# A feed-forward's row of 1/rms(x): spread over the partitions by two TensorE matmuls instead of two DMAs through DRAM, with the first gates issued one group of column tiles earlier

## The chip, the cores and the metric

The kernel runs on one core of one Trainium2 chip. The metric is the device time of one execution in microseconds (us); three runs of the kernel before gave a median of 2030.98 us. A difference is called one only when it is above about 0.2% of that.

## The reference

The reference is a trunk of four layers on x of 256 tokens x 1024 features. Each layer is a half-step SwiGLU feed-forward, a token mixer and another half-step feed-forward. Mixers alternate: chunked attention (layers 0 and 3), a gated MLP (layer 1), differential attention (layer 2). All is float32. The part that matters here is the feed-forward, which occurs eight times:

```python
def rms_norm(x, g):
    y = xf * lax.rsqrt(jnp.mean(xf * xf, axis=-1, keepdims=True) + EPS)
    return (y * g.astype(jnp.float32)).astype(x.dtype)
def swiglu(h, w_in, w_out):            # w_in 1024 x 5632, w_out 2816 x 1024
    gate, up = jnp.split(h @ w_in, 2, axis=-1)
    return (jax.nn.silu(gate) * up) @ w_out
x = x + 0.5 * rms_norm(swiglu(rms_norm(x, g[0]), ff1_w_in[i], ff1_w_out[i]), g[1])
```

## The kernel before, in words

**Layout.** x lies in SBUF transposed: features on the 128 partitions in 8 tiles (`KD`), 256 tokens along the columns. A product h @ w is made column tile by column tile: the weights (128 x 128 blocks) are the stationary operand, h with 256 columns the moving one. To keep float32 accuracy with the fast float32r type, each operand is split into a high and a low part and three matmuls are made for each block: high x high, high x low, low x high.

**The weights' stream** (class `Stream`, lines 87 to 161). Weights come in the order of use in chunks of 1 MB (tile `w_raw`, three buffers, DMAs issued on SP, line 104). A chunk holds two *pieces*; a piece is one column tile for all 8 k, 8 blocks. Each piece is split: ScalarE (ACT) casts its high part `w_hi` (line 127) and VectorE (DVE) subtracts to give its low part `w_lo` (line 130); the low part of a piece is issued only when the next piece is split (`settle`). Eight buffers of split pieces exist. `W.done(n, most)` says that n pieces were used and lets the stream split up to `most` further pieces, so that a piece is normally split eight pieces ahead of its use. A chunk's DMA is issued when the chunk three earlier has had both its pieces split. Between two branches the stream is held (`hold`, `resume`); in front of a feed-forward that follows a mixer it has split three pieces fewer than in front of one that follows another feed-forward.

**Order.** TensorE, DVE and ACT run their instructions in the order in which the program issues them (`manual_schedule`); a wait at the head of one of them holds back everything behind it on that engine. So the place of a call in the program sets the order.

**The norm.** `Normed` (line 248) multiplies x by the gain only; the factor 1/rms(x), one number per token, is applied later, to the products. `sums` (line 321) makes the sums of squares with small matmuls (`column_sums`, line 225), a square root on ACT (line 233) and a reciprocal on DVE (line 235); the result `rs` has tokens on the partitions, 128 x 2. The products have tokens along the columns, so the factor must be spread as a row over all partitions (tile `rbc`). There are two ways. `spread` (line 327) transposes and broadcasts by matmuls with the identity (`spread2`, line 240) into PSUM and copies the row to SBUF on ACT (line 331); attention uses it. `spread_later` (line 333) writes the 256 numbers to DRAM (tile `row`, line 337) and reads them back onto all 128 partitions (line 338), both DMAs issued on POOL; the feed-forward and the gated MLP use it.

**The feed-forward** (`ffn`, line 511). The first product has 22 gate tiles and 22 up tiles. The loop over `jp` (0 to 10) takes a group of two gate and two up tiles, i = 0 to 3, in `project_pair` (line 471): 24 matmuls for each i, 96 for a group (group 0, after an update of x, is made in another order, line 482, and partly ahead). A group's results fill one PSUM tile `pp_t` of a pool with three buffers, so group 3 can only start when `gate` of group 0 has read the buffer. After the matmuls of each i, `between(i)` is called and then `W.done(1, 2)`, which issues the splits of further pieces.

`gate` (line 521) is a chain of five instructions: DVE multiplies the gate tiles by `rbc` (line 523), ACT applies Silu (line 524), DVE multiplies by the up tiles, which is the last read of the PSUM tile (line 526), ACT casts the high part of the hidden layer (line 528) and DVE makes the low part (line 529). The second product (lines 551 to 563) follows the loop.

In the kernel before, `sums` and `spread_later` are called in group 1 after i = 0; groups 0 and 1 are kept in `held`, and their gates are issued in group 2 after i = 1 and i = 2. From group 2 on each gate is issued right after its group.

Of the kernel before, what the change touches and what calls it, by code (L numbers as in the profile page):

```python
# [16 lines left out]
P = 128  # L17
# [19 lines left out]
# an input that comes in tile by tile: its high parts, and a tile later its low parts  # L37


def _order(ks):  # L40
    """The products' two steps for each k, the one of the input's low part a k behind."""
    steps = [(k, low) for k in ks for low in (False, True)]
    for i in range(1, len(steps) - 1, 2):
        steps[i], steps[i + 1] = steps[i + 1], steps[i]
    return steps
# [3 lines left out]
# After an update of x: first the tiles of which nothing is made ahead.  # L49
# [7 lines left out]
def encoder_trunk_kernel(  # L57
# [29 lines left out]
    class Stream:  # L87
        """Chunks of 16 blocks (128 x 128) in the order of use; a piece is half a chunk."""
# [43 lines left out]
        def settle(self):  # L132
            # the low part follows a piece later, so that its engine need not wait for the high part
            if self.pending:
                self.low(*self.pending)
                self.pending = None
# [74 lines left out]
    class Warm:  # L211
        """Matmuls whose result nobody reads, to keep the tensor engine's clock up while it waits."""
# [17 lines left out]
    def inv_sqrt(src, bias, n, scale):  # L230
        """1 / sqrt(scale * src + bias) of n columns."""
        sd = small.tile([P, n], F32, tag=f"sd{n}", name="sd")
        nc.scalar.activation(sd, src, AF.Sqrt, bias=bias, scale=scale)
        r = small.tile([P, n], F32, tag=f"rs{n}", name="rs")
        nc.vector.reciprocal(r, sd)
        return r

    def spread(col, ps):
        # ps[p, t] = col[t] on every partition p
        nc.tensor.matmul(ps, col.broadcast_to([P, P]), ident, start=True, stop=True)  # L240
# [7 lines left out]
    class Normed:  # L248
        """x * gain in float32r parts, with 1/rms(x) kept aside, per token."""
# [35 lines left out]
        def begin(self, gain):  # L285
            """x itself comes in, and with it the first weights."""
            for k in range(KD):
                self.high(gain, k, k + 1)
                self.low(gain, k, k + 1)
                if k == 0:  # L290
                    W.split()
            for i in range(3):
                W.split()
                W.settle()
                for a in ((0, 2, 4), (6,), ())[i]:
                    self.square(a)
            self.total()
# [29 lines left out]
        def spread(self):  # L327
            """The same on all partitions, for tokens along the columns."""
            ps = spread2(self.tok)
            self.bc = tmp.tile([P, S], F32, tag="rbc", name="rbc", bufs=1)  # L330
            nc.scalar.copy(self.bc, ps)

        def spread_later(self):
            """The same by way of DRAM, where it may take some microseconds."""
            row = dram.tile([S], F32, tag="row", name="row")
            self.bc = tmp.tile([P, S], F32, tag="rbc", name="rbc", bufs=1)
            nc.gpsimd.dma_start(row.rearrange("(h p) -> p h", h=2), self.tok)
            nc.gpsimd.dma_start(self.bc, row.unsqueeze(0).broadcast_to([P, S]))

    class Branch:  # L340
        """A branch's output y, tile by tile: y * gain, and the sum of squares."""

        def __init__(self, gain, n=None, ahead=None):
            """n: the normed input whose 1/rms y still lacks; eps then goes with the square of that rms."""
            self.gain, self.n, self.ahead = gain, n, ahead
# [23 lines left out]
        def finish(self):  # L369
            """The updates of x."""  # L370
            f = inv_sqrt(self.ss[:, 0:2], eps2_t if self.n else eps_t, 2, 1.0 / D)
            self.fill(8)
            fb = spread2(f)
            self.fill(36 if self.ahead else 12)
            return Update(self.yg, f, fb, self.ahead)

    class Ahead:
        """Some of the next products, of x and of y apart, made while y's factor f is on its way: (x + f y) w."""
# [28 lines left out]
        def begin(self):  # L407
            """The first tile of the next products, and apart from it y's share."""
            self.ps, self.share = pair(), bank()
            for o, xs in ((self.ps[:, 0, :], self.x), (self.share, self.y)):  # L410
                for k in self.ks:
                    if self.wide:
                        wh, wl = [part.rearrange("p (k c) -> p k c", k=2)[:, k % 2, :] for part in W.peek(k // 2)]
                    else:
                        wh, wl = [part[:, k, :] for part in blocks(W.peek())]
                    for m, (w_, h) in enumerate(((wh, 0), (wl, 0), (wh, 1))):
                        x = xs[k][:, h, :]
                        first, last = (k, m) == (self.ks[0], 0), (k, m) == (self.ks[-1], 2)
                        self.todo.append((o, w_, x, first, last and o is self.share))
# [10 lines left out]
        def scale(self, update):  # L430
            """y's share, times the factor."""
# [12 lines left out]
    class Update:  # L444
        """x += y * factor, tile by tile."""
# [16 lines left out]
    def large(tag, shape, dtype=F32):  # L462
        """A part of the two arrays of the feed-forward's hidden layer, or what a mixer keeps there."""
        t = act.tile([P, LARGE[tag]], dtype, tag=tag, name=tag)
        n = math.prod(shape)
        return t[:, 0:n].rearrange("p (a b) -> p a b", a=shape[0]) if len(shape) > 1 else t[:, 0:n]
# [4 lines left out]
    def project_pair(n, together, between=lambda piece: None, finish=lambda ps: None, most=2, warm=None):  # L471
        """Two tiles of two column sets each; all four at once where the input comes in k by k."""
# [38 lines left out]
    def ffn(l, which, update, ahead):  # L511
# [21 lines left out]
        def between(jp):  # L533
            def at(i):
                if jp == 1 and i == 0:
                    n.sums(AF.Silu)
                    n.spread_later()
                if jp == 2 and i > 0 and held:
# [3 lines left out]
        for jp in range(NJ // 2):  # L542
            ps = project_pair(n, jp == 0 and not first, between(jp), **(dict(most=1, warm=Warm()) if first and jp == 0 else {}))
            if jp < 2:
# [23 lines left out]
    def project_out(parts, l, between, ahead):  # L568
        """y = o @ w. parts(k): o's float32r parts; between(k): what else is to be done before the k-th is used."""
# [33 lines left out]
    def joined(early, outs):  # L603
        """The float32r parts of a mixer's output, tiles 0 to 3 and 4 to 7 in different places."""
# [4 lines left out]
    class Wide:  # L609
        """Columns of h @ w with tokens on the partitions, 512 columns at a time, a piece (2 of 8 k) per step."""  # L610
# [35 lines left out]
    # Columns of a map: queries 0-127 x keys 0-127, queries 128-255 x keys 128-255, queries 128-255 x keys 0-127.  # L646
# [20 lines left out]
    def soft_exp(s, scale):  # L667
        """exp(scale * (s - max)) for each row of each map, and their sums: [P, map, query half]."""
# [20 lines left out]
    def transpose_probs(p, dst):  # L689
        """p's blocks -> keys 0-127 x queries 0-255, keys 128-255 x queries 128-255."""  # L690
# [5 lines left out]
    def attention(n, softmax, transposes, v_done, mix, prepare=lambda: None, soon=lambda: None):  # L696
        """v's first half, q and k, the maps of each two tiles, and v's other half, with no wait of the tensor engine."""
# [17 lines left out]
        def quarter(i, j):  # L715
            # while the projections of the next two tiles, or of v, go on
# [43 lines left out]
    def mixer_a(l, i, update):  # L760
# [65 lines left out]
        def mix(j):  # L826
            # the heads of v's first 512 columns while the others are made
# [6 lines left out]
        def between(k):  # L834
            # the rest of the heads while the first ones' share of the output is made
# [18 lines left out]
    def mixer_b(l, i, update):  # L854
# [56 lines left out]
        def mix(jp):  # L911
            # rows of v mixed in their chunk, for two of the groups
# [46 lines left out]
    def mixer_c(l, i, update):  # L959
# [9 lines left out]
        # |q - k| on the blocks  # L969
# [7 lines left out]
        # lambda  # L977
# [18 lines left out]
        def softmax(h, sc):  # L996
# [8 lines left out]
            def finish():  # L1005
                # the first map's sums stay in, and come out with the norm: its eps takes their squares
# [21 lines left out]
        def apply(g):  # L1028
            # two heads, tokens on the partitions
# [14 lines left out]
        def summed(g):  # L1044
            # the sums of its squares
# [5 lines left out]
        def normed(g):  # L1051
            # the group over its root mean squares
# [18 lines left out]
        def mix(j):  # L1071
            # the heads of v's first 512 columns while the others are made
# [11 lines left out]
        def between(k):  # L1084
            # the rest of the heads while the first ones' share of the output is made
# [40 lines left out]
def _lay_out(i):  # L1126
    """The inputs in the order in which the chip reads them."""
# [5 lines left out]
    def narrow(w):  # L1133
        # [1024, 1024] -> chunks of two column tiles: [p, 2 * k * 128]
        return w.reshape(KD, P, KD // 2, 2, P).transpose(2, 1, 3, 0, 4).reshape(-1, P, WC)

    def wide(w):
        # [1024, 1024] -> chunks (column half, k half): [p, 4 * 512]
        return w.reshape(2, 4, P, 2, 512).transpose(3, 0, 2, 1, 4).reshape(-1, P, WC)

    def two(w, tiles):
        # [1024, 2 * tiles * 128] -> chunks of a tile of either half: [p, 2 * k * 128]
        return w.reshape(KD, P, 2, tiles, P).transpose(3, 1, 2, 0, 4).reshape(-1, P, WC)

    def deep(w):
        # [2816, 1024] -> blocks (column tile, k), 16 to a chunk
# [17 lines left out]
    # relative-position bias, Toeplitz: same 128-block, and the block before  # L1164
# [34 lines left out]
```

## Time and profile before

| | |
|---|---|
| median of three runs (lowest to highest) | 2030.98 us (2030.81 to 2031.15) |
| span of the profiled execution | 2036.8 us |
| ACT busy, DVE busy | 1076.5 us (53%), 1276.6 us (63%) |
| POOL busy | 16.9 us (1%) |
| mean granted TensorE clock | 0.989 |
| HBM read | 348.49 MB, 172 GB/s over the span |

The profile is one execution taken by the hardware profiler. Its page gives the busy time of each engine (PE is TensorE's matmuls, PEld its weight loads), the chain of work that ended last, groups of instructions by line, and DMAs by size and time to landing. The trace behind it can be asked for waits (who waited for whom), for a timeline of single instructions (start, duration, and in brackets the idle time before and who ended it), and for stretches of time (busy time of each engine, granted clock, busy share of the 16 DMA engines, GB/s). A matmul's shown duration includes its way through the pipeline; the pace of a series of matmuls is read from their starts.

### The profile page before, as it was taken

How to read it: one execution, taken by the hardware profiler on the slowest of the kernel's cores; microseconds unless marked ns; L12 is line 12 of the kernel's file. 1: busy time of each engine (PE TensorE's matmuls, PEld its weight loads, DVE VectorE, ACT ScalarE, POOL GpSimd, SP SyncE). 2: the span in 40 equal slices, each digit the busy share in tenths (PEclk: the TensorE clock that was granted, in tenths of full speed). 3: DMA queues.
4: the chain of work that ended last, by engine and by line, in shares of the span. 5: the costliest groups of instructions: out<-in, count | busy, mean ns of one | idle time of the engine just before them, and what ended most of it. 6: DMA issues, size and time to landing. Idle time of an engine off the chain costs nothing.

```text
span 2036.8 us, 37668 instructions
## 1 busy us (share of the span) xinstructions
PE 1986.9 (98%) x16195; PEld 1956.4 (96%) x16195; DVE 1276.6 (63%) x1689; ACT 1076.5 (53%) x1602; POOL 16.9 (1%) x37
## 2 busy tenths in 40 slices
PE   8999999899999999899999999989999999998998
PEld 8999999899999989899999999989999999998998
DVE  5655766655565567655666558766556655866653
ACT  5554665545454555545554555754545455565442
POOL 0000000000000000000000000000000000000000
PEclk9999999999999999999999999999999999999999
DMA  8545525554554553654464544265447454526541
GB/s 252 187 186 188 188 102 144 214 202 169 146 209 182 191 168 125 192 204 174 158 188 182 191 148 166 104 185 204 174 146 196 186 198 166 188 104 170 199 193 42
DMA packets 51142, 351.96 MB, mean 173 GB/s; under 512 B 6144, under 2 KB 6400, under 8 KB 9760
## 3 DMA queue, kind: packets, MB, share of 16 engines
q1 hardware_dynamic: 48096, 341.86, 48.7%
q10 hardware_dynamic: 2160, 6.52, 0.9%
q8 instruction: 126, 2.06, 0.4%
q0 software_dynamic: 720, 1.19, 0.3%
q14 instruction: 40, 0.33, 0.0%
HBM read 348.49 MB, written 1.06 MB: 172 GB/s over the span
## 4 chain that ended last, share of the span: by engine, by line
PE 88%; DMA 6%; DVE 3%; ACT 2%; issue 1%; ACTq 0%; SPq 0%; DVEq 0%
PE pp_t L501 46%; PE pp_t L166 9%; PE pp_t L168 9%; PE pp_t L167 9%; DMA w_raw<-in_w 6%; PE pp_t L482 3%; PE pp_t L621 3%; PE pp_t L579 2%; DVE w_lo L130 1%; ACT w_hi L127 1%; PE pp_t L661 1%; PE pp_t L427 1%; PE pst_t L693 1%; PE pst_t L427 1%; PE pst_t L225 1%
## 5 line engine op out<-in xcount | busy, mean ns | idle before, releaser
L127 ACT CAST w_hi<-w_raw 128x1024 fp32r<-128x1024 f32 (+1 forms) x649 | 668.2, 1047 | 545.9 <-PE pp_t L501 242.2
L130 DVE TENSOR_TENSOR w_lo<-w_raw,w_hi 128x1024 fp32r<-128x1024 f32 (+1 forms) x649 | 773.5, 1218 | 272.0 <-ACT w_hi L127 254.0
L501 PE MATMUL pp_t<-xh,w_hi 128*128 128x256 f32 x2976 | 533.2, 286 | 35.2 <-DVE hf L526 33.9
L501 PE MATMUL pp_t<-xl,w_hi 128*128 128x256 f32 x2976 | 529.1, 285 | 0.2 <-DVE xl L316 0.2
L501 PE MATMUL pp_t<-xh,w_lo 128*128 128x256 f32 x2976 | 528.6, 285 | 0.0
L501 PEld LDWEIGHTS pp_t<-xh,w_hi 128*128 128x128 f32 x2976 | 435.7, 194 | 38.3 <-issue 35.3
L501 PEld LDWEIGHTS pp_t<-xl,w_hi 128*128 128x128 f32 x2976 | 436.0, 194 | 0.5 <-DVE xl L316 0.4
L501 PEld LDWEIGHTS pp_t<-xh,w_lo 128*128 128x128 f32 x2976 | 435.8, 194 | 0.1
L166 PE MATMUL pp_t<-h,w_hi 128*128 128x256 f32 x1456 | 412.1, 283 | 0.0
L167 PE MATMUL pp_t<-h,w_lo 128*128 128x256 f32 x1456 | 412.1, 283 | 0.0
L168 PE MATMUL pp_t<-l,w_hi 128*128 128x256 f32 x1440 | 407.6, 283 | 0.0
L167 PEld LDWEIGHTS pp_t<-h,w_lo 128*128 128x128 f32 x1456 | 279.6, 192 | 0.0
L166 PEld LDWEIGHTS pp_t<-h,w_hi 128*128 128x128 f32 x1456 | 279.6, 192 | 0.0
L168 PEld LDWEIGHTS pp_t<-l,w_hi 128*128 128x128 f32 x1440 | 276.5, 192 | 0.0
L363 DVE TENSOR_TENSOR ysq<-ysq,sq 128x256 f32<-128x256 f32 x72 | 30.5, 424 | 128.4 <-ACT sq L352 128.3
L523 DVE TENSOR_TENSOR gs<-pp_t,rbc 128x512 f32<-128x512 f32 x88 | 60.5, 688 | 77.7 <-PE pp_t L501 77.7
L526 DVE TENSOR_TENSOR hf<-pp_t,gs 128x512 f32<-128x512 f32 x88 | 60.9, 692 | 68.1 <-ACT gs L524 68.1
L524 ACT ACTIVATE gs<-gs 128x512 f32<-128x512 f32 x88 | 55.6, 632 | 84.0 <-DVE gs L523 84.0
L529 DVE TENSOR_TENSOR l<-hf,h 128x512 fp32r<-128x512 f32 x88 | 60.9, 692 | 60.4 <-ACT h L528 60.4
L528 ACT CAST h<-hf 128x512 fp32r<-128x512 f32 x88 | 54.5, 620 | 66.6 <-DVE hf L526 66.6
L301 ACT ACTIVATE xh<-xr,g_sb 128x256 fp32r<-128x256 f32 x96 | 44.8, 504 | 59.0 <-DVE xr L458 56.4
L678 ACT ACTIVATE ex<-s,nm 128x128 f32<-128x128 f32 x96 | 42.7, 448 | 43.5 <-DVE nm L670 25.3
(191 smaller groups left out, 1706.4 us busy)
## 6 DMA issues: line engine op xcount, KB each, us to landing
w_raw<-in_w SPq DMA_DIRECT2D x322, 1024.0 KB, 4.9
l<-in_a_bias ACTq DMA_DIRECT2D x8, 512.0 KB, 7.5
w_raw<-in_w SPq DMA_DIRECT2D x3, 512.0 KB, 7.2
rbc<-row POOLq DMA_DIRECT2D x9, 128.0 KB, 7.3
out_y<-xr SPq DMA_DIRECT2D x4, 256.0 KB, 2.5
xr<-in_x_t SPq DMA_DIRECT2D x2, 384.0 KB, 5.4
w_raw<-in_w SPq DMA_DIRECT2D x2, 256.0 KB, 4.4
l<-in_b_ws ACTq DMA_DIRECT2D x1, 512.0 KB, 5.4
```

What stands on the lines that cost most here:

```text
L127: nc.scalar.copy(hi[:, cols], raw[:, cols])
L130: nc.vector.tensor_tensor(lo[:, cols], raw[:, cols], hi[:, cols].bitcast(F32), op=ALU.subtract)
L166: nc.tensor.matmul(o, ah, bh, start=start, stop=False, skip_group_check=skip)
L167: nc.tensor.matmul(o, al, bh, start=False, stop=False, skip_group_check=skip)
L168: nc.tensor.matmul(o, ah, bl, start=False, stop=stop, skip_group_check=skip)
L482: nc.tensor.matmul(o, part[:, k, :], (n.l if low else n.h)[:, k, :], start=((k, low) == JOIN[0] and i == 2 and part is ws[i][0]), stop=((k ...
L501: nc.tensor.matmul(o, part[:, k, :], xs[:, k, :], start=(at == 0), stop=(at == 3 * KD - 1))
L523: nc.vector.tensor_tensor(gs, ps[:, :, 0:S], n.bc.unsqueeze(1).broadcast_to([P, 2, S]), op=ALU.mult)
L524: nc.scalar.activation(gs, gs, AF.Silu)
L526: nc.vector.tensor_tensor(hf, ps[:, :, S:2 * S], gs, op=ALU.mult)
L529: nc.vector.tensor_tensor(hl, hf, hh.bitcast(F32), op=ALU.subtract)
L621: nc.tensor.matmul(self.ps[:, t, :], xs[:, kk, t * P:(t + 1) * P], ws, start=((kk, low) == self.order[0] and ws is wh and not (t == 0 and ...
```

## The change

In the feed-forward alone, `spread` takes the place of `spread_later`, one i later, in group 1; the gate of group 0 is issued in group 1 after i = 2; the gate of group 1 is issued right after its group, as all later ones are. The gated MLP keeps `spread_later`. The diff's other lines take out comments and docstrings and are left out here; a line of the changed kernel behind line 537 stands one lower than before.

```diff
         def between(jp):
             def at(i):
                 if jp == 1 and i == 0:
                     n.sums(AF.Silu)
-                    n.spread_later()
-                if jp == 2 and i > 0 and held:
+                if jp == 1 and i == 1:
+                    n.spread()
+                if jp == 1 and i == 2:
                     gate(*held.pop(0))
             return at
...
             ps = project_pair(n, jp == 0 and not first, between(jp), **(dict(most=1, warm=Warm()) if first and jp == 0 else {}))
-            if jp < 2:
+            if jp == 0:
                 held.append((jp, ps))
             else:
                 gate(jp, ps)
```

The two helpers that change places, unchanged themselves:

```python
        def spread(self):
            ps = spread2(self.tok)      # two matmuls into PSUM: ps[p, t] = tok[t] on every p
            self.bc = tmp.tile([P, S], F32, tag="rbc", name="rbc", bufs=1)
            nc.scalar.copy(self.bc, ps)

        def spread_later(self):
            row = dram.tile([S], F32, tag="row", name="row")
            self.bc = tmp.tile([P, S], F32, tag="rbc", name="rbc", bufs=1)
            nc.gpsimd.dma_start(row.rearrange("(h p) -> p h", h=2), self.tok)
            nc.gpsimd.dma_start(self.bc, row.unsqueeze(0).broadcast_to([P, S]))
```

## The prediction, made before the changed kernel was run

> **What bounds the kernel now.** I read the page first, then the waits of TensorE.
>
> ```profile
> PE 1986.9 (98%) x16195; PEld 1956.4 (96%) x16195; DVE 1276.6 (63%) x1689; ACT 1076.5 (53%) x1602; POOL 16.9 (1%) x37
> ```
> ```profile
> PE pp_t L501 <- DVE hf L526: 33.9, 8, 6.9
> ```
> ```profile
> PE pp_t L501 <- ACT w_hi L127: 1.3, 1, 1.3
> ```
>
> The first row says that TensorE sets the time almost everywhere, so an edit is worth what it takes out of or puts into TensorE's row. The second (us in total, times, longest) is nearly all of TensorE's idle time: eight waits, one for each feed-forward, for line 526, the last read of a group's PSUM tile. Group 3 waits for group 0's buffer. The third is the only wait of these products for a weight, 1.3 us at the kernel's start.
>
> Next, why line 526 is late: the timeline of one feed-forward (layer 1's second), TensorE, then ACT, then DVE; start, duration, idle time before in brackets.
>
> ```profile
> 819.66 1.12 PE L501 MATMUL pp_t<-xh,w_lo 128*128 128x256 f32 x8
> 820.62 1.12 PE L501 MATMUL pp_t<-xh,w_hi 128*128 128x256 f32 x8
> ```
> ```profile
> 836.94 1.12 PE L501 MATMUL pp_t<-xh,w_lo 128*128 128x256 f32 x8
> 843.30 0.55 PE L501 MATMUL pp_t<-xh,w_hi 128*128 128x256 f32 x1 [5.25 <-DVE hf L526]
> ```
> ```profile
> 819.41 2.94 ACT L127 CAST w_hi<-w_raw 128x1024 fp32r<-128x1024 f32 x3
> 822.60 2.00 ACT L127 CAST w_hi<-w_raw 128x1024 fp32r<-128x1024 f32 x2 [0.25 <-DMA w_raw<-in_w]
> 834.15 2.00 ACT L127 CAST w_hi<-w_raw 128x1024 fp32r<-128x1024 f32 x2 [9.55 <-DMA w_raw<-in_w]
> 837.73 1.99 ACT L127 CAST w_hi<-w_raw 128x1024 fp32r<-128x1024 f32 x2 [1.59 <-DMA w_raw<-in_w]
> 840.22 1.04 ACT L127 CAST w_hi<-w_raw 128x1024 fp32r<-128x1024 f32 x1 [0.50 <-DMA w_raw<-in_w]
> 841.80 0.63 ACT L524 ACTIVATE gs<-gs 128x512 f32<-128x512 f32 x1 [0.54 <-DVE gs L523]
> ```
> ```profile
> 818.13 0.17 DVE L235 RECIPROCAL rs<-sd 128x2 f32<-128x2 f32 x1 [0.38 <-ACT sd L233]
> ...
> 820.49 5.77 DVE L130 TENSOR_TENSOR w_lo<-w_raw,w_hi 128x1024 fp32r<-128x1024 f32 x5 [1.08 <-ACT w_hi L127]
> ```
> ```profile
> 842.46 0.69 DVE L526 TENSOR_TENSOR hf<-pp_t,gs 128x512 f32<-128x512 f32 x1 [0.69 <-ACT gs L524]
> ```
>
> A step of TensorE takes 0.12 us (eight from 819.66 to 820.62). Groups 1 and 2 run without a gap until 836.94 + 0.96 = 837.90. Group 0's products were there before group 1 began, but its Silu stands on ACT behind twelve casts of weights (two ahead of these rows), the last five of which waited for DMA; 842.46 + 0.69 = 843.15 frees the buffer. Gate 0 is held by its place in the queue, behind weights that TensorE does not need yet.
>
> Why were the weights late there? Stretches of time (the last three columns: granted clock, DMA busy share, GB/s), with a stretch of the first attention, which spreads its row by matmuls:
>
> ```profile
> 822.00:825.00 3.00, 3.00 (x27) 3.00 (x27) 3.00 (x3) 2.35 (x3) 0.00 (x0) 1.00 1.46 44
> 825.00:828.00 3.00, 3.00 (x27) 3.00 (x27) 1.26 (x2) 0.00 (x0) 0.00 (x0) 1.00 0.90 41
> 828.00:831.00 3.00, 3.00 (x27) 3.00 (x27) 0.00 (x0) 0.00 (x0) 0.57 (x1) 1.00 0.54 27
> 831.00:834.00 3.00, 3.00 (x27) 3.00 (x27) 0.00 (x0) 0.00 (x0) 0.00 (x0) 1.00 0.79 330
> ```
> ```profile
> 226.00:229.00 3.00, 3.00 (x27) 3.00 (x27) 1.60 (x2) 3.00 (x5) 0.91 (x3) 1.00 1.05 430
> ```
> ```profile
> rbc<-row POOLq DMA_DIRECT2D x9, 128.0 KB, 7.3
> ```
> ```profile
> row<-rs POOLq DMA_DIRECT2D x9, 1.0 KB, 10.4
> ```
> ```profile
> 824.02 13.62 DMA w_raw<-in_w
> ```
>
> For nine us the DMA engines move 27 to 44 GB/s, busy as they are. In that time the row is written to DRAM: 1 KB, 10.4 us to land, as 256 pieces of 4 bytes by its access pattern. A 1 MB chunk issued into it takes 13.62 us. So the row's write probably holds the weights up; the read back starts only after it.
>
> **The change part by part.** *Gate 0 earlier.* In the new order ACT and DVE meet it after the casts of group 1's i = 0 and 1, ahead of the first cast that waits long for DMA. Step by step in this feed-forward: `rs` is there at 818.13 + 0.17 = 818.30; the spread's matmuls stand after i = 1, at 820.62, 2.3 us later, so TensorE does not wait for them. ACT's copy lies between two casts at about 821.4. The next casts end near 823.8, as DVE's low parts do (820.49 plus three of 5.77/5 = 1.15). Then line 523 (about 0.69), Silu 0.63, line 526 0.69: the buffer is free near 826.0, needed at 838.3 (837.90 plus the spread's own time, below). Cover: 12 us. The wait goes altogether.
>
> *What is queued behind gate 0.* The next piece's cast and two low parts move back by the chain, about 3.5 us. The nearest use is the low part of the fourth piece split in group 1, due in the last third of group 2's i = 2: 826.38 is group 2's start (837.90 less 96 steps of 0.12), plus 5.76 + 1.92 + the spread's 0.44 = 834.5; it is made by 828.6. Slack 5.9 us. One chunk's issue moves back as much; its pieces are for group 4, over 20 us later. *Gate 1* now follows the casts of four more pieces on ACT. Even if the DMA stays clogged as above it would run at about 840, and its buffer is needed 11.5 us after 838.3. Covered in both cases. Gate 2 keeps its place.
>
> *What is late next.* With no pause, group 3 needs its first pieces at 838.3. Even clogged, they were cast from 834.15 on, and a low part takes 1.15 us more; unclogged they come earlier by up to 9 us. The two shortest of the eight pauses now:
>
> ```profile
> 561.32 0.35 PE L501 MATMUL pp_t<-xh,w_hi 128*128 128x256 f32 x1 [1.16 <-DVE hf L526]
> ```
> ```profile
> 1552.80 0.36 PE L501 MATMUL pp_t<-xh,w_hi 128*128 128x256 f32 x1 [1.40 <-DVE hf L526]
> ```
>
> No wait for weights follows them. So I take nothing as late next.
>
> *The gain.* Idle 33.9 us. The idle time counts from the modelled end of the last matmul (836.94 + 1.12 = 838.06), not from when the next was due (837.90): 0.16 x 8 = 1.3. Then the clock after the pause. The 768 matmuls of groups 3 to 10, in the chain of waits, the first, a quick one, that behind a pause of 2.09 us, and the last of eight:
>
> ```profile
> 48.45 94.01 PE pp_t L501 x768
> ...
> 561.32 92.38 PE pp_t L501 x768
> ...
> 1041.07 93.87 PE pp_t L501 x768
> ...
> 1867.17 94.27 PE pp_t L501 x768
> ```
> ```profile
> 1041.07 0.36 PE L501 MATMUL pp_t<-xh,w_hi 128*128 128x256 f32 x1 [2.09 <-DVE hf L526]
> ```
> ```profile
> 1042.07:1043.07 1.00, 1.00 (x7) 1.00 (x6) 1.00 (x2) 0.46 (x1) 0.00 (x0) 0.50 0.11 41
> ```
>
> 92.38 is the time at full clock (0.12 us a step). The last row is the stretch right behind that pause, granted clock in the third column from its end. All eight sum to 749.95; less 8 x 92.38 = 739.04 leaves 10.9 us lost at a clock granted at 0.50 behind six of the pauses, the 2.09 us one among them. Gain: 33.9 + 1.3 + 10.9 = 46.1.
>
> By the Trainium skill (TensorE: Matmul & The Clock Gate, The HAM clock gate) the clock halves only after an idle window of about 3.4 us, in a window that runs free. By that rule the 2.09 us pause would cost no clock, and 1.5 us (93.87 less 92.38) would go from the 10.9. The trace disagrees: 0.50 behind 2.09 us. I keep 10.9.
>
> *The cost.* The first attention's spread:
>
> ```profile
> 226.18 0.60 PE L240 MATMUL pst_t<-ident,rs 128*128 128x128 f32 x4
> 226.54 1.20 PE L501 MATMUL pp_t<-xh,w_hi 128*128 128x256 f32 x8
> 227.58 1.12 PE L501 MATMUL pp_t<-xl,w_hi 128*128 128x256 f32 x8
> ```
>
> 226.18 to 227.58 is 1.40 us, of which eight steps of 0.12 are 0.96: 0.44 us of TensorE each (two matmuls, four passes), 3.5 for eight. The copy is hidden by ACT's wait for DMA; if the cover were gone it would move casts, not TensorE, for the slack above. POOL loses its two DMA issues, and nothing of the feed-forward waits there.
>
> *Sum.* 46.1 - 3.5 = 42.6 off the profiled execution: 2036.8 to 1994.2. The median is 5.8 us below that span, and no row says where the 5.8 us lie. If outside the waits, the median goes to 2030.98 - 42.6 = 1988.4; if all inside the waits (the unprofiled kernel pausing less), to 1994.2. I take 1988, as the waits have a cause in the program that does not need the profiler.
>
> **The rivals.** *Part of the pause comes back as waits for weights.* The four feed-forwards behind a mixer and the first one start with fewer pieces split. If something else than the row clogs the DMA (the stream's restart), the pauses of up to 6.9 us, which now let the stream catch up, would be missing. Half the gain would remain: 2030.98 - 21.3 = 2009.7. For it: the stream restarts in the same microseconds. Against it: attention restarts its stream at 430 GB/s without a DRAM row.
>
> *Gate 0 in front of casts that are needed sooner* (slower). If the copy of the row lands on ACT behind a cast that waits for a chunk, gate 0 and everything behind it wait as long. It costs from 5.9 us of delay on, and makes the kernel slower from 5.9 + 42.6/8 = 11.2 us. At the 13.62 us of the chunk above: 7.7 idle and about 1.9 of half clock, x 8 = 77 - 43 = 34 slower: 2065. Against it: the casts ahead of the copy waited at most 0.25 us in these rows.
>
> *The change does not do what it says*: something else holds the buffer as long, and only the matmuls are added: 2030.98 + 3.5 = 2034.5.
>
> **How the numbers follow.** All pauses gone: 0.83, 1984 to 1994 (low end: the spread free, 3.5; high end: the 5.8 us). Part back: 0.11, 1994 to 2015. Slower: 0.03. No effect: 0.03. The range 1983 to 2000 takes the first case and the near part of the second, and the 1.5 us of clock phase either way. About 0.2% (4 us) can be told from no change: faster 0.94, same 0.03, slower 0.03.
>
> **What would show it.** TensorE's waits: the row for line 526 gone, no new row for `w_hi` or `w_lo` in line 501; granted clock 1.00 through groups 3 and 4; eight runs of 768 near 92.4 us; line 240's matmuls 32 more (8 x 4 passes), no `row` in the feed-forwards; no stretch under 50 GB/s after the sums. Wrong: a wait of line 240 for `rs`, a wait of line 501 for weights, or GB/s that still fall there.

## The result, and the profile after

| | kernel before | changed kernel | ratio (95% interval) |
|---|---|---|---|
| first session, median | 2030.89 us (2030.81 to 2031.15) | 1995.19 us (1993.93 to 1996.56) | 0.9823 (0.9809 to 0.9837) |
| a later session, median | 2036.85 us (2034.90 to 2041.35) | 1996.46 us (1996.33 to 1998.04) | 0.9801 (0.9787 to 0.9814) |
| span of the profiled execution | 2036.8 us | 1992.1 us | |

The forecast was 1988 us, range 1983 to 2000. Off the medians went 35.7 and 40.4 us, off the profiled spans 44.7, against 42.6 in the sum.

The page of the changed kernel, busy time and share of the span, and then the engines' shares of the chain that ended last:

```profile
PE 1978.3 (99%) x16227; PEld 1949.1 (98%) x16227; DVE 1279.4 (64%) x1689; ACT 1081.5 (54%) x1610; POOL 6.5 (0%) x21
...
PE 97%; DVE 1%; DMA 1%; ACT 1%; issue 0%; ACTq 0%; SPq 0%; DVEq 0%
```

TensorE has 32 matmuls more (16227 less 16195) and is the chain for 97% of the span. All of its waits above 0.5 us (who waited for whom; us in total, times, longest):

```profile
PE pp_t L918 <- DVE l L910: 3.0, 1, 3.0
PE pp_t L219 <- DVE filler L198: 1.3, 1, 1.3
PE pp_t L166 <- DVE us L936: 0.8, 1, 0.8
PE pp_t L501 <- ACT w_hi L127: 0.7, 1, 0.7
```

The row for line 526 is gone, and no wait for weights has taken its place. Lines 918 and 166 are the gated MLP, which still writes its row to DRAM.

The same feed-forward as in the prediction (layer 1's second, whose group 1 now begins 16.7 us sooner), ACT and then DVE:

```profile
804.66 0.37 ACT L331 COPY rbc<-pst_t 128x256 f32<-128x256 f32 x1
804.92 2.05 ACT L127 CAST w_hi<-w_raw 128x1024 fp32r<-128x1024 f32 x2
807.98 0.63 ACT L524 ACTIVATE gs<-gs 128x512 f32<-128x512 f32 x1 [1.01 <-DVE gs L523]
809.37 0.62 ACT L528 CAST h<-hf 128x512 fp32r<-128x512 f32 x1 [0.76 <-DVE hf L526]
809.89 3.91 ACT L127 CAST w_hi<-w_raw 128x1024 fp32r<-128x1024 f32 x4
```
```profile
808.64 0.69 DVE L526 TENSOR_TENSOR hf<-pp_t,gs 128x512 f32<-128x512 f32 x1 [0.70 <-ACT gs L524]
```

Read the last column first: no cast here waits for DMA. Silu of gate 0 stands behind six casts instead of twelve. Its buffer is free at 808.64 + 0.69 = 809.33. Stretches behind the sums of this feed-forward (granted clock, DMA busy share, GB/s at the end of each row); then, from the chain of waits, three of its eight stretches of 912 matmuls (group 1 from i = 2 on, and groups 2 to 10), the middle one that of this feed-forward; then TensorE at the start of group 3:

```profile
805.00:808.00 3.00, 3.00 (x27) 3.00 (x26) 2.94 (x4) 1.99 (x4) 0.00 (x0) 1.00 0.67 221
808.00:811.00 3.00, 3.00 (x27) 3.00 (x26) 1.68 (x3) 2.24 (x4) 0.00 (x0) 1.00 1.03 423
811.00:814.00 3.00, 3.00 (x27) 3.00 (x26) 3.00 (x3) 2.80 (x3) 0.00 (x0) 1.00 0.36 109
```
```profile
26.79 109.44 PE pp_t L501 x912
...
804.57 109.44 PE pp_t L501 x912
...
1807.79 109.44 PE pp_t L501 x912
```
```profile
821.68 0.28 PE L501 MATMUL pp_t<-xh,w_hi 128*128 128x256 f32 x1
```

221, 423 and 109 GB/s stand where 27 to 44 stood; in the last of these rows the DMA engines are busy for a share of only 0.36, so there is little to load and nothing is held up. All eight feed-forwards now have one unbroken chain of 912 matmuls in 109.44 us, 0.12 us each: no pause, no half clock. Group 3 starts at 821.68, 12.3 us behind the free buffer.

### The profile page after: what moved, and what is told of

Read it like the earlier page. It is cut to its first block, busy times and chain, and to the rows that moved or that the text cites. A ratio compares the mean times of both kernels' runs of the same rounds, so it can differ in the third digit from the quotient of the medians.

```text
span 1992.1 us, 37700 instructions
## 1 busy us (share of the span) xinstructions
PE 1978.3 (99%) x16227; PEld 1949.1 (98%) x16227; DVE 1279.4 (64%) x1689; ACT 1081.5 (54%) x1610; POOL 6.5 (0%) x21
## 4 chain that ended last, share of the span: by engine, by line
PE 97%; DVE 1%; DMA 1%; ACT 1%; issue 0%; ACTq 0%; SPq 0%; DVEq 0%
PE pp_t L501 54%; PE pp_t L166 9%; PE pp_t L168 9%; PE pp_t L167 9%; PE pp_t L482 3%; PE pp_t L622 3%; PE pp_t L580 2%; PE pp_t L662 1%; DMA w_raw<-in_w 1%; PE pp_t L427 1%; PE pst_t L694 1%; PE pst_t L427 1%; PE pst_t L225 1%; PE pst_t L240 1%; PE pp_t L425 0%; PE pp_t L816 0%
## 5 line engine op out<-in xcount | busy, mean ns | idle before, releaser
L501 PE MATMUL pp_t<-xh,w_hi 128*128 128x256 f32 x2976 | 527.7, 284 | 0.7 <-ACT w_hi L127 0.7
L501 PEld LDWEIGHTS pp_t<-xh,w_hi 128*128 128x128 f32 x2976 | 430.1, 192 | 2.6 <-ACT w_hi L127 1.4
L501 PEld LDWEIGHTS pp_t<-xl,w_hi 128*128 128x128 f32 x2976 | 430.7, 192 | 0.7 <-DVE xl L316 0.4
L501 PEld LDWEIGHTS pp_t<-xh,w_lo 128*128 128x128 f32 x2976 | 430.7, 192 | 0.1
```

Of the source, the lines that this page charges most:

```text
L501: nc.tensor.matmul(o, part[:, k, :], xs[:, k, :], start=(at == 0), stop=(at == 3 * KD - 1))
```

## The experiments

The main theory in the expectations is called C: the row's write clogs the DMA engines, so casts of weights come late, and gate 0 stands behind them.

**The kernel before again.** No edit.

> The kernel before, unchanged, profiled and timed once more. The profiled execution of before had a span of 2036.8 us, 5.8 us over the median of the timed runs, while every run of the changed kernel is 1.8 us longer than its span. Theory P (the pauses vary from execution to execution, and the profiled one had long ones): a second profile shows another sum of the waits for line 526 than 33.9 us (26 to 33), with a span lower by that and by the half clock that goes with it, and the rest of the stages as before. Theory O (the 5.8 us lie outside the pauses): the eight waits sum to 33.9 us again within 1 us, and a stage without pause differs.

Median 2037.23 us; profiled span 2034.1, in which TensorE's waits for line 526 are:

```profile
PE pp_t L501 <- DVE hf L526: 30.4, 8, 5.9
```

30.4 instead of 33.9, in an execution 2.7 us shorter; the half clock behind the pauses cost as much as before (the eight chains of 768 matmuls sum to 750.12 us here, and to 749.95 in the first profile). The kernel's runs spread from 2034.2 to 2042.2 us beside one another. Theory P holds as far as it goes: the pauses differ from execution to execution. No profile was taken of an execution near the first session's 2031, so that its pauses were shorter is argued and not shown.

**The spread alone, gates in their old places.**

```diff
                 if jp == 1 and i == 1:
                     n.spread()
-                if jp == 1 and i == 2:
+                if jp == 2 and i > 0 and held:
                     gate(*held.pop(0))
...
-            if jp == 0:
+            if jp < 2:
```

> Half the change: the row is spread by matmuls, but gates 0 and 1 stay where they were, in group 2. Theory C (the row's write to DRAM clogs the DMA engines, so that the casts ahead of gate 0 wait for weights): no stretch under 50 GB/s behind the sums, casts wait for DMA by under 2 us each, gate 0's last read ends near group 2's end, pauses of 0 to 1 us each; 1994 to 2003 us. Theory Q (the pause is only the queue order, the restart of the weights' stream is slow by itself): the pauses stay, 30 us and more in sum, and the time is that of before plus 3.5 us for the matmuls, 2030 to 2036.

1997.40 us, ratio 0.9802 (0.9782 to 0.9822): all of the gain, within what can be told. ACT in the same feed-forward, the last cast ahead of gate 0, and gate 0's Silu:

```profile
822.35 1.05 ACT L127 CAST w_hi<-w_raw 128x1024 fp32r<-128x1024 f32 x1 [0.69 <-DMA w_raw<-in_w]
823.72 0.63 ACT L524 ACTIVATE gs<-gs 128x512 f32<-128x512 f32 x1 [0.32 <-DVE gs L523]
```
```profile
827.83 0.28 PE L501 MATMUL pp_t<-xh,w_hi 128*128 128x256 f32 x1
```

The last row is the start of group 3, which waits for nothing. In its old place the Silu ends at 824.35, line 526 at about 825.1: in time by some 2.8 us, as the casts ahead of it wait only 1.91, 1.48 and 0.69 us for weights. (Over all feed-forwards one such wait is longer than the 2 us expected: 3.29 us.) No wait for line 526 is left in the trace. Theory Q falls.

**The early gates alone, the row through DRAM.**

```diff
                 if jp == 1 and i == 0:
                     n.sums(AF.Silu)
-                if jp == 1 and i == 1:
-                    n.spread()
+                    n.spread_later()
```

> The other half: the row goes through DRAM as before, but gate 0 stands in group 1 behind i = 2 and gate 1 behind its group. Theory C: the row is back some 18 us after the sums, gate 0 waits for it at the head of DVE and ACT, the low parts of weights behind it come late, and TensorE waits for weights in group 2 instead of for the buffer in group 3, by 4 to 8 us in the five feed-forwards that start with fewer pieces split and under 2 us in the other three; 2015 to 2045 us. Theory Q (order alone is enough): no pause, no matmuls added, 1988 to 1995 us.

2038.63 us, ratio 1.0004 (0.9991 to 1.0016): no gain. TensorE's waits, and DVE where gate 0 begins:

```profile
PE pp_t L501 <- DVE w_lo L130: 32.5, 5, 7.7
```
```profile
835.93 0.69 DVE L523 TENSOR_TENSOR gs<-pp_t,rbc 128x512 f32<-128x512 f32 x1 [12.63 <-DMA rbc<-row]
```

Gate 0 now holds the head of DVE for 12.63 us until its row is back, the low parts of the weights queue behind it, and TensorE waits for those: five times, for 3.6 to 7.7 us, in the five feed-forwards of the expectation. The pause has changed its name and its group, and kept its size.

**The changed kernel with the row still written beside it.**

```diff
+        def row_only(self):
+            row = dram.tile([S], F32, tag="row", name="row")
+            nc.gpsimd.dma_start(row.rearrange("(h p) -> p h", h=2), self.tok)
...
                     n.sums(AF.Silu)
+                    n.row_only()
```

> The changed kernel, and beside it the 1 KB row is still written to DRAM in every feed-forward, in the same pieces; nothing reads it. Theory C: the stretches under 50 GB/s are back for 6 to 9 us, casts of group 1's later pieces wait 8 to 10 us for DMA again, but with gate 0 ahead of them TensorE waits for nothing: the changed kernel's time plus 0 to 3 us, 1994 to 1999. Theory R (without a pause the weights of groups 3 and 4 come late when the DMA is clogged): waits of line 501 for weights of 2 us and more in several feed-forwards, 2003 to 2015 us. If the write is harmless, GB/s stay above 100 in these stretches.

1996.55 us, ratio 0.9798 (0.9777 to 0.9819), where the changed kernel had 0.9801 in a later session. Stretches, and ACT (lines of this kernel stand four lower):

```profile
810.00:813.00 3.00, 3.00 (x27) 3.00 (x26) 2.21 (x3) 1.56 (x3) 0.00 (x0) 1.00 1.32 44
813.00:816.00 3.00, 3.00 (x27) 3.00 (x26) 2.41 (x3) 1.50 (x2) 0.00 (x0) 1.00 0.92 33
```
```profile
811.55 0.63 ACT L528 ACTIVATE gs<-gs 128x512 f32<-128x512 f32 x1 [0.68 <-DVE gs L527]
...
820.97 2.00 ACT L127 CAST w_hi<-w_raw 128x1024 fp32r<-128x1024 f32 x2 [6.46 <-DMA w_raw<-in_w]
```

The clog is back and a cast waits 6.46 us (6.4 to 7.5 in seven of the eight feed-forwards, a little under the 8 to 10 expected). But gate 0 is already through, and TensorE waits for no weight beyond 0.7 us at the kernel's start, as in the changed kernel. So the rival of the prediction, that pauses come back as waits for weights, falls even with the DMA clogged.

**The same write with the gates in their old places.** The edits of the second and the fourth experiment together: matmul spread, late gates, unread write.

> Matmul spread, gates 0 and 1 in their old places in group 2, and the 1 KB row still written to DRAM beside it; nothing reads it. Theory C (the write holds up the weights, and gate 0 stands behind their casts): the eight pauses are back though gate 0's own input is there early, 25 to 34 us in waits for line 526; 2030 to 2044 us. Rival T (gate 0 was late because its row came back late): no pauses, 1995 to 2000 us, as with the spread alone.

2032.18 us, ratio 0.9973 (0.9963 to 0.9983). TensorE's waits, and ACT:

```profile
PE pp_t L505 <- DVE hf L530: 25.3, 8, 5.4
```
```profile
822.90 0.37 ACT L331 COPY rbc<-pst_t 128x256 f32<-128x256 f32 x1
823.16 3.05 ACT L127 CAST w_hi<-w_raw 128x1024 fp32r<-128x1024 f32 x3
835.53 2.00 ACT L127 CAST w_hi<-w_raw 128x1024 fp32r<-128x1024 f32 x2 [9.32 <-DMA w_raw<-in_w]
838.07 2.00 ACT L127 CAST w_hi<-w_raw 128x1024 fp32r<-128x1024 f32 x2 [0.54 <-DMA w_raw<-in_w]
841.81 1.04 ACT L127 CAST w_hi<-w_raw 128x1024 fp32r<-128x1024 f32 x1 [1.73 <-DMA w_raw<-in_w]
842.76 0.62 ACT L528 ACTIVATE gs<-gs 128x512 f32<-128x512 f32 x1
```

This settles the cause. Gate 0's own input is there at 823.27, its Silu runs at 842.76, held by casts that wait for DMA. A write of 1 KB in each feed-forward that nobody reads costs 34.8 us over the spread alone (1997.40; that run is of the session before, in which the kernel before had 2037.57 us, and 2036.85 in this one). Rival T falls. The pauses are somewhat shorter than the 30.4 and 33.9 us of the kernel before. Of the way through DRAM only the read back of the row is missing here; what it adds was not measured by itself.

**The changed kernel again.** No edit.

> The changed kernel once more, beside runs of the kernel before in the same session. The forecast took 42.6 us off; the first session measured 35.7 off the medians and 44.7 off the profiled spans. Theory P (the kernel before differs from session to session by how long its pauses are, the changed one has none and so differs less): 1993 to 1998 us here, 39 to 44 us under the kernel before. Theory O (a part of the change's time is not seen in profiles): again 36 us under the kernel before, 2000 to 2003 if that is at 2037 to 2039.

1996.46 us, 40.4 under the kernel before; the changed kernel moved by 1.3 us between the sessions, the kernel before by 6.0. That is what theory P expects; why the kernel before was quicker in the first session it does not show.

**Five spreads in place of one.**

```diff
                 if jp == 1 and i == 1:
-                    n.spread()
+                    for _ in range(5):
+                        ps = spread2(n.tok)
+                    n.bc = tmp.tile([P, S], F32, tag="rbc", name="rbc", bufs=1)
+                    nc.scalar.copy(n.bc, ps)
```

> The changed kernel with each feed-forward's spread made five times over, one behind the other, the last one used. It prices the matmuls: the four added pairs cost 0.36 us each by the starts of the row quoted (0.44 with the slow start of what follows, which is paid once): 8 x 4 x 0.36 = 11.5 to 14.1 us over the changed kernel, 2006 to 2010 us if that is at 1995. If they lay beside other work: 0.

2011.66 us, ratio 0.9874 (0.9861 to 0.9888), 15.2 us over the changed kernel of the same session: 32 pairs more, 0.475 us each. TensorE in one feed-forward:

```profile
336.08 2.39 PE L240 MATMUL pst_t<-ident,rs 128*128 128x128 f32 x20
338.23 1.20 PE L501 MATMUL pp_t<-xh,w_hi 128*128 128x256 f32 x8
```

Five pairs take from 336.08 to 338.23, 2.15 us or 0.43 each, on TensorE's path in full; one pair took 0.36 by the prediction's row (226.18 to 226.54). So the four added cost 1.79 us, 14.3 for eight feed-forwards. That and the 15.2 measured are a little over the 11.5 to 14.1 expected; the 0.9 between them is within the spread of the changed kernel's runs.

**The gated MLP's row by matmuls too.**

```diff
         def between(q):
             if q == 0:
                 n.sums(AF.Gelu)
-                n.spread_later()
             if q == 1:
+                n.spread()
                 v_done(0, ps_v)
```

> The changed kernel with the gated MLP's row spread by matmuls too, one step later than its sums. Theory C: the stretch under 50 GB/s behind the MLP's sums goes, the cast behind it that waits some 11 us for DMA comes at once, and of TensorE's two waits there (3.0 and 0.8 us) most goes: 2.5 to 4 us less in that stage, less 0.44 for the matmuls; 1990 to 1994 us if the changed kernel is at 1995. Rival: these waits are for DVE's own chain (normalise), they stay, and the time is the changed kernel's within 1 us.

1989.15 us (1988.94 to 1989.36), ratio 0.9764 (0.9751 to 0.9778), 7.3 us under the changed kernel of its session: the fastest version here. The cast that decides, in the changed kernel of that session and then in this one:

```profile
740.13 1.05 ACT L127 CAST w_hi<-w_raw 128x1024 fp32r<-128x1024 f32 x1 [9.93 <-DMA w_raw<-in_w]
```
```profile
729.29 1.05 ACT L127 CAST w_hi<-w_raw 128x1024 fp32r<-128x1024 f32 x1 [0.69 <-DMA w_raw<-in_w]
```

The rival falls: none of these waits is left. More went than the 2.5 to 4 us expected. The expectation was read from a profile with a short clog (the cast waited 6.97 us there, not 11; TensorE waited 3.0 and 0.8 us), and it left out the clock: 3.4 us at a granted clock of 0.50 stand behind these waits there, and none in this version. Priced like the half clock behind the prediction's pause of 2.09 us (93.87 less 92.38, 1.5 us), that makes 3.0 + 0.8 + 1.5 - 0.44 = 4.9 us, and the profiled spans, 1992.1 and 1987.2, differ by 4.9. In the profile of the later session TensorE waited longer, 3.1, 1.4 and 1.1 us, and the spans differ by 9.0. Runs of this version lie within 0.4 us of each other, those of the changed kernel within 1.7 and 2.6: the last row written to DRAM probably made most of its scatter.

**What about the write clogs: its pieces or its queue.** An unread write beside the changed kernel, cut in four ways: layer 0 as before, 256 pieces of 4 bytes; layer 1, 128 of 8; layer 2, 128 of 4; layer 3, 1 KB in one piece. Issued on POOL:

```diff
+            if l == 0:
+                nc.gpsimd.dma_start(row.rearrange("(h p) -> p h", h=2), self.tok)
+            elif l == 1:
+                nc.gpsimd.dma_start(row.rearrange("(p h) -> p h", h=2), self.tok)
+            elif l == 2:
+                nc.gpsimd.dma_start(row[0:P].rearrange("(p h) -> p h", h=1), self.tok[:, 0:1])
+            else:
+                nc.gpsimd.dma_start(row.unsqueeze(0), self.acc[0:1, 0, :])
```

> The changed kernel with an unread write to DRAM beside it in each feed-forward, cut in four ways: layer 0 as in the kernel before (256 pieces of 4 bytes), layer 1 128 pieces of 8 bytes, layer 2 128 pieces of 4 bytes (half the row), layer 3 one piece of 1 KB (a row of the sums of squares instead of the factors). Theory N (each piece occupies a DMA engine for about the same time): 10 us to land in layer 0, 5 to 7 in layers 1 and 2, 2 to 3 in layer 3, and the casts' wait for DMA behind it shrinks alike. Theory S (what costs is the byte count or the write to DRAM as such): about 10 us in all four. Theory B (only pieces of 4 bytes are slow): layer 1 is quick, layer 2 is not.

The trace's times from issue to landing, layers 0 to 3, two feed-forwards each:

```profile
DMA to landing us min/median/max: 10.0/10.3/10.7
```
```profile
DMA to landing us min/median/max: 4.2/5.6/6.9
```
```profile
DMA to landing us min/median/max: 8.5/9.6/10.8
```
```profile
DMA to landing us min/median/max: 1.6/1.8/2.0
```

Halving the number of 4-byte pieces changes little, and doubling their size to 8 bytes nearly halves the time. The longest wait of a cast for weights behind the write is 6.5, 2.5, 5.9 and 0.6 us in layers 0 to 3: one piece clogs nothing. That the layers differ in other ways is not the reason, as 256 pieces of 4 bytes took 9.6 us or more in every layer of the fourth experiment. Theory S falls, N holds only in part, and B fits best; two feed-forwards for each cut leave its finer form open. On ACT's queue, the same cuts with the call moved behind i = 1:

> The same four writes, issued on ACT's queue (hardware descriptors) and one step later instead of on POOL's. Theory N (the pieces cost, whoever issues them): landing times as in the run on POOL's queue within 2 us, and the weights held up as long. Theory K (POOL's way of issuing is what is slow): 2 to 4 us to land in all layers, no stretch under 50 GB/s.

```profile
DMA to landing us min/median/max: 11.1/11.1/11.1
```

That is layer 0 (one run of each of these two kernels: 1998.82 and 1998.06 us beside 2038.38); layer 1 took 4.2 and 6.7 us, layer 2 7.8. Stretches at 14 to 55 GB/s stood behind the writes of these three layers, and casts waited up to 6.6, 2.7 and 6.0 us, as on POOL. Theory K falls. Only one landing each is recorded for layers 0 and 2, and none for layer 3.

The Trainium skill (DMA: Bandwidth & Descriptors, Specifications) gives 512 bytes as the least transfer for full rate, with a read, modify and write below it. The runs agree in direction, 1.8 us for one piece of 1 KB against 10.3 for 256 of 4 bytes; no run here shows the read, modify and write itself.

## Why the prediction was right, point by point

- **The eight pauses go**: right. The order of events came as worked out: buffer free 12.3 us ahead of need (forecast 12), the casts ahead of the copy without a wait.
- **The clock**: right. With the pauses the 10.9 us of half clock went; the eight chains run at 0.12 us a step throughout. That a pause of 2.09 us costs clock was the better of the two readings, by the granted clock of 0.50 in its row; the time alone could not have told 10.9 us from 9.4.
- **The matmuls' price**: right. 0.44 us was taken; five in a row measure 0.43 each in the trace, and the added ones 0.475 by the medians.
- **The row's write holds the weights up**: it stood as "probably" and is shown by the two unread writes. What the prediction gave to gate 0's early place was too much: with the clog gone the old place is early enough (1997.40 us), though by some 2.8 us and not 12. The early place is a second safeguard: of these experiments it is needed only in those in which something still clogs the DMA (1996.55 with it, 2032.18 without).
- **Nothing is late next**: right, and so also under the clog.
- **Not in the sum**: the gated MLP's own waits shrank in the profiled execution after, where its row landed in 7.5 us instead of 8.6, from 3.1, 1.1 and 0.6 us to 3.0 and 0.8; the wait for a weight at the kernel's start went from 1.3 to 0.7. These make 1.6 of the 2.1 us by which the spans differ more than forecast.
- **The mis-sized term** is the choice between 1988.4 and 1994.2: "I take 1988, as the waits have a cause in the program". The cause is in the program, but the size of the waits is the clog's, which differs between executions. Measured were 1995.2 and 1996.5, beyond both: all pauses went, and yet the time lies over the 1994 at which the prediction ends that case. It is within the range because the range reaches to 2000. One error is plain. The 5.8 us come from a run's time set beside a span, but each run of the changed kernel takes 1.8 to 1.9 us more than its span, and each later run of the kernel before 1.7 to 2.9. So a median of 2031 goes with a span of 2028 to 2029, some 8 us under the profiled one. The other error is that the gain was taken off a time to which it did not belong: off the profiled execution's own time, 2036.8 + 1.8, the 42.6 us lead to 1996.0. That the first session's runs paused less is the likely reading and is not shown: they lie within 0.4 us of each other, and none of the 45 later runs of the kernel before came under 2034.2. So something differs between sessions, and not only between executions; what it is stays open.

## What to carry to other kernels

A tiny DMA can cost more than a large one, as the row of 1 KB in 256 pieces did here: before asking whether its result is needed late enough, look at the GB/s of the stretch in which it runs and at who else's data arrives there. When TensorE waits for a buffer, follow its reader's queue back to the first instruction that waited for something: here the remedy lay there (the weights) and not at the reader. And take a gain from the profile off the profile's own time, with the same kind of time on both sides (span or run): if the runs scatter where the lost time sits, the median before may not contain all of it.

## What the runs showed of the hardware

- 256 writes of 4 bytes to DRAM, 1 KB in all, took 7.5 to 11.6 us over all the runs looked at, on POOL's queue and on ACT's alike. In the feed-forwards they held 1 MB loads on another queue down to 14 to 68 GB/s for most of that time. 1 KB in one piece landed in 1.6 to 2.0 us.
- In three traces (the kernel before twice, and the write with the old gates) each pause of TensorE at the head of group 3 that was 2.09 us or longer was followed by a stretch at a granted clock of 0.50, 3.4 us of it behind the one of 2.09 us. None of the pauses of up to 1.54 us was; between the two lengths none was seen.
